# Two outputs by stream at stages' ends, and first outputs one stream after the other, in a two-layer diffusion block

## The chip, the core and the metric

The kernel runs on one core of one Trainium2 chip. The metric is device microseconds for one launch; the median over runs is compared. Engines are named as in the profile: PE is the matrix engine (PEld its weight loads), DVE the vector engine, ACT the scalar engine, POOL the general engine, SP the engine that issues most transfers.

## The reference, cut to what matters

Two layers of a diffusion backbone over 256 context tokens (stream 0) and 256 latent tokens (stream 1), with width 1024. Each layer is a gated feed-forward half step, a mixing step (retention, windowed attention and a recurrent branch, merged and projected) and a second feed-forward half step. Each of the three starts with an RMS norm and a modulation by stream:

```python
def rms_norm(x, w, eps=NORM_EPS):
    xf = x.astype(jnp.float32)
    y = xf * lax.rsqrt(jnp.mean(jnp.square(xf), -1, keepdims=True) + eps)
    return (y * w.astype(jnp.float32)).astype(x.dtype)
def modulate(h, shift, scale):
    return h * (1.0 + scale) + shift
def swiglu(h, w_in, w_out):
    gate, up = jnp.split(h @ w_in, 2, axis=-1)
    return (jax.nn.silu(gate) * up) @ w_out
def ffn_sublayer(x, mod, base, norm_w, w_in, w_out):
    h = modulate(rms_norm(x, norm_w), mod[:, :, base], mod[:, :, base + 1])
    return x + 0.5 * mod[:, :, base + 2] * swiglu(h, w_in, w_out)
```

The output is the latent stream after layer 1.

## The kernel before, in words

Features lie on partitions in 8 tiles of 128 (`KT` = 8); the 512 columns are stream 0 (0 to 255) and stream 1 (256 to 511). A product in float32 is three matmuls on split operands (`mm3`, L185 to L188): high weights by high input, high weights by low input, low weights by high input.

Weights come in tiles of four 128x128 blocks, in the order of a plan (`plan_ffn`, `plan_mix`) that also packs them in memory. `Weights.get` fetches a tile of 256 KB by SP (L113), casts the high part on ACT (L114) and subtracts for the low part on DVE (L115). It keeps the current tile and the one before it; who asks for an older one has it fetched again.

`body` runs three stages for each layer: ffn1 (weights `w0a`, `w1a`), mix (`w0b`, `w1b`) and ffn2 (`w0c`, `w1c`). Both streams go through all of them, but for layer 1's ffn2 and the outputs of its mix, which are latent alone. So four stage ends hand both streams on, and the text calls them E1 (ffn1 to mix in layer 0), E2 (mix to ffn2 in layer 0), E3 (ffn2 of layer 0 to ffn1 of layer 1) and E4 (ffn1 to mix in layer 1).

At a stage's end the last of 8 output tiles goes by stream (`last_out`): 33 matmuls of 256 columns for a stream in a feed-forward stage, 24 in the mix. After each comes the residual on DVE (L373) and the square of that tile (L276). `stats` sums squares by matmuls of one column (L283), takes a root in small DVE steps (L286, L194 to L203) and broadcasts the result over 128 rows by transposes (L290): for stream 0 into `ps_rf`, for stream 1 into `ps_po`. `norm` then makes the inputs of the next stage, for each tile of features and each stream three instructions: u on DVE (L300), the high part of the input on ACT (L302) and the low part on DVE (L303). It takes stream 0's tile kt and then stream 1's tile kt-2.

`first` makes a stage's first outputs (6 tiles in a feed-forward stage, 3 low-rank tiles "lo" in the mix, of which stream 0 of layer 1 has 2) as the inputs come: for each tile of features stream 0's part and, one tile behind, stream 1's with the same weights (L364 with the high input, L369 with the low one).

At the mix's start ACT also casts low-rank weights (`lora`, fetched at L847, cast at L850), whose fetch is held until the last tile of x has been stored (`xd`, L1249).

Each engine's order is not written out: a scheduler with its own timeline model sets it (`TileContext(auto_bufs=True, schedule_with_timeline_sim=True)`).

Of the kernel before, what the change touches and what calls it, by code (L numbers as in the profile page):

```python
# [38 lines left out]
def plan_ffn(wi, wo):  # L39
    out = []  # L40
    for hf in range(2):
        if hf == 0:
            out.append(("first", [(wi, kt, n + p) for kt in range(KT) for p in range(G3) for n in (0, FT)]))
# [3 lines left out]
        for n in range(KT):  # L47
            out.append((f"o{hf}.{n}", fm(wo, n, HF, hf * HF)))
# [9 lines left out]
def plan_mix(l):  # L58
    r0 = RCOL // 128
    out = []  # L60
    for w in ORDER[l].split():
        k, j = w[0], w[1:]
        if w == "lo":
            out.append(("lo", [("mix", kt, r0 + 12 + j) for kt in range(KT) for j in range(3)]))
# [20 lines left out]
    out += [(f"wo{n}", fm("wout", n)) for n in range(KT)]  # L85
    return out
# [36 lines left out]
def body(nc, tc, I, O, es, dbg=None):  # L123
# [684 lines left out]
    def rw_lora(W, H, l, S, st):  # L808
# [4 lines left out]
        first(W, "lo", H, cs, os, 1, 1)  # L813
# [389 lines left out]
    def mix_out(l, W, ms, S, xd):  # L1203
# [21 lines left out]
    for l in range(2):  # L1225
# [15 lines left out]
        W = Weights(nc, mk, I[f"w{l}a"], plan_ffn("f1i", "f1o"))  # L1241
# [17 lines left out]
        W = Weights(nc, mk, I[f"w{l}c"], plan_ffn("f2i", "f2o"))  # L1259
# [49 lines left out]
def arrange(x, c, ctx, c_ctx, ada_w, ada_b, norm_w, ffn1_w_in, ffn1_w_out, ffn2_w_in, ffn2_w_out, mix_w_in,  # L1309
# [55 lines left out]
```

## Time and profile before

| what | value |
|---|---|
| median of 3 runs | 2956.5 us (2952.3 to 2960.07) |
| profiled execution, its own time | 2952.92 us |
| span of its trace | 2951.1 us |
| granted clock of TensorE, mean | 0.963 |
| weight tiles fetched, cast and split | 954 |

The busy shares of the page are averages over the whole span. The change touches four short stretches and the mix behind two of them, so the rows further down are those of the stretches from the end of a stage's last matmul to the last matmul of the next stage's first outputs.

### The profile page before, as it was taken

To read this page: it belongs to the slowest core of one execution; us is meant where nothing else is said; L and a number is where in the kernel's file an instruction comes from. 1 tells how busy PE (TensorE), PEld (TensorE's weight loads), DVE (VectorE), ACT (ScalarE), POOL (GpSimd) and SP (SyncE) were. 2 spreads that over 40 slices of the span, in tenths; PEclk is the share of its full clock that TensorE was granted. 3 is DMA by queue.
4 is the path that set the end of the run, shared out by engine and by line. 5 is a ranking of instruction groups with operands and counts; after the bars stand their busy time and mean duration, and the time that the engine had idled before them with its cause. 6 is when DMAs were issued, how large, how long until landed. Compare 5 with 4: busy or idle time off the path is not lost.

```text
span 2951.1 us, 47422 instructions
## 1 busy us (share of the span) xinstructions
PE 2796.3 (95%) x16761; PEld 2387.8 (81%) x16761; DVE 1999.8 (68%) x4677; ACT 1320.8 (45%) x2968; POOL 375.0 (13%) x1068
## 2 busy tenths in 40 slices
PE   8999999889999999899999999999989898999999
PEld 7888888677877787688888888888878787888999
DVE  7967668666685766467746567455787776577655
ACT  3322245556555654333223332223467665564544
POOL 0000000522032211000000000000033433330000
PEclk9999999889999999999999999999999999799999
DMA  7656444212332146433534435353334233146554
GB/s 268 232 188 192 155 127 132 76 49 82 115 97 78 50 128 216 154 104 126 184 136 162 145 121 173 108 174 120 123 109 112 80 114 113 53 131 202 171 179 154
DMA packets 259727, 400.97 MB, mean 136 GB/s; under 512 B 78752, under 2 KB 96288, under 8 KB 259488
## 3 DMA queue, kind: packets, MB, share of 16 engines
q1 hardware_dynamic: 259488, 397.93, 42.5%
q8 instruction: 132, 2.16, 0.3%
q14 instruction: 107, 0.88, 0.1%
HBM read 368.33 MB, written 25.82 MB: 134 GB/s over the span
## 4 chain that ended last, share of the span: by engine, by line
PE 79%; DVE 6%; POOL 5%; DMA 4%; ACT 2%; issue 2%; SPq 1%; POOLq 0%; DVEq 0%; ACTq 0%
PE ps_mm L186 20%; PE ps_mm L188 20%; PE ps_mm L187 20%; POOL cst L1007 3%; POOL cst L1006 2%; PE ps_mm L364 2%; PE ps_po L774 1%; PE ps_rf L974 1%; DVE wlo L115 1%; PE ps_rx L1084 1%; DMA z<-td 1%; PE ps_po L559 1%; PE ps_rx L1077 1%; PE ps_rx L364 1%; PE ps_rx L1105 1%
## 5 line engine op out<-in xcount | busy, mean ns | idle before, releaser
L114 ACT CAST whi<-raw 128x512 fp32r<-128x512 f32 x954 | 564.6, 617 | 698.9 <-PE ps_mm L187 362.4
L186 PE MATMUL ps_mm<-hall,whi 128*128 128x512 f32 (+1 forms) x2320 | 841.6, 363 | 5.7 <-DVE ft L693 1.5
L188 PE MATMUL ps_mm<-hall,wlo 128*128 128x512 f32 (+1 forms) x2320 | 841.1, 363 | 2.3 <-DVE wlo L115 2.2
L187 PE MATMUL ps_mm<-hall,whi 128*128 128x512 f32 (+1 forms) x2320 | 838.3, 362 | 0.0
L115 DVE TENSOR_TENSOR wlo<-raw,whi 128x512 fp32r<-128x512 f32 x954 | 645.5, 692 | 98.2 <-ACT whi L114 68.4
L186 PEld LDWEIGHTS ps_mm<-hall,whi 128*128 128x128 f32 x2320 | 440.8, 190 | 75.2 <-ACT kv L711 2.0
L188 PEld LDWEIGHTS ps_mm<-hall,wlo 128*128 128x128 f32 x2320 | 439.0, 189 | 75.9 <-DVE wlo L115 4.7
L187 PEld LDWEIGHTS ps_mm<-hall,whi 128*128 128x128 f32 x2320 | 439.7, 190 | 71.3 <-issue 0.3
L186 PE MATMUL ps_mm<-hid,whi 128*128 128x512 f32 (+1 forms) x737 | 260.7, 354 | 0.0
L187 PE MATMUL ps_mm<-hid,whi 128*128 128x512 f32 (+1 forms) x737 | 259.9, 354 | 0.0
L188 PE MATMUL ps_mm<-hid,wlo 128*128 128x512 f32 (+1 forms) x737 | 257.4, 354 | 0.0
L1006 POOL TENSOR_TENSOR cst<-acc,cst 128x60 f32<-128x60 f32 (+24 forms) x496 | 167.9, 339 | 613.7 <-DMA acc<-ad__10934 59.4
L373 DVE SCALAR_TENSOR_TENSOR x<-ps_mm,cst,x 128x256 f32<-128x256 f32 x136 | 61.0, 481 | 193.7 <-PE ps_mm L188 193.6
L401 DVE TENSOR_TENSOR ft<-ft,ps_mm 128x512 f32<-128x512 f32 (+1 forms) x80 | 49.6, 621 | 209.0 <-PE ps_mm L188 199.4
L851 POOL TENSOR_TENSOR ll<-lora,lh 128x512 fp32r<-128x512 f32 x8 | 10.5, 1316 | 1367.9 <-DMA cst<-gup 953.9
L1007 POOL TENSOR_TENSOR cst<-cst 128x60 f32<-128x60 f32 (+24 forms) x496 | 177.2, 357 | 38.0
L236 DVE SCALAR_TENSOR_TENSOR ft<-m,cd 128x1024 bf16<-128x1024 f32 x136 | 163.0, 1221 | 8.7 <-DMA m<-ada 8.7
L237 DVE SCALAR_TENSOR_TENSOR m<-m,cd 128x1024 f32<-128x1024 f32 x136 | 165.6, 1223 | 0.7
L187 PEld LDWEIGHTS ps_mm<-hid,whi 128*128 128x128 f32 x737 | 139.1, 189 | 19.5
L186 PEld LDWEIGHTS ps_mm<-hid,whi 128*128 128x128 f32 x737 | 139.0, 189 | 19.4
L188 PEld LDWEIGHTS ps_mm<-hid,wlo 128*128 128x128 f32 x737 | 138.5, 189 | 19.5
L186 PE MATMUL ps_mm<-whi,hall 128*128 128x256 f32 x416 | 120.7, 291 | 8.2 <-DVE rr_v L799 5.1
(339 smaller groups left out, 4518.7 us busy)
## 6 DMA issues: line engine op xcount, KB each, us to landing
m<-ada SPq DMA_DIRECT2D x136, 512.0 KB, 4.3
raw<-w0b SPq DMA_DIRECT2D x214, 256.0 KB, 2.9
raw<-w1b SPq DMA_DIRECT2D x211, 256.0 KB, 3.1
raw<-w0a SPq DMA_DIRECT2D x132, 256.0 KB, 2.8
raw<-w0c SPq DMA_DIRECT2D x132, 256.0 KB, 4.4
raw<-w1a SPq DMA_DIRECT2D x132, 256.0 KB, 4.3
raw<-w1c SPq DMA_DIRECT2D x132, 256.0 KB, 3.9
gd<-ft SPq DMA_DIRECT2D x24, 256.0 KB, 2.0
```

Source lines behind the costliest of these rows:

```text
L114: nc.scalar.copy(hi, raw)
L115: nc.vector.tensor_sub(lo, raw, hi.bitcast(F32))
L186: PE.matmul(o, w[0], h[0], start=start, stop=False)
L187: PE.matmul(o, w[0], h[1], start=False, stop=False)
L188: PE.matmul(o, w[1], h[0], start=False, stop=stop)
L236: V.scalar_tensor_tensor(junk, raw, 1.0, st["cond"][0], ALU.mult, ALU.mult, accum_out=md[:, kt, 0:1])
L237: V.scalar_tensor_tensor(raw, raw, 1.0, st["cond"][1], ALU.mult, ALU.mult, accum_out=md[:, kt, 1:2])
L364: PE.matmul(o[:, p], w[k, j][q], hl(H[k], p)[0], start=(k == 0 and q == 0 and p.start == c.start), stop=False)
L373: V.scalar_tensor_tensor(xs[n][:, CS[s]], o[:, CS[s]], gate[:, n, s:s + 1], xs[n][:, CS[s]], ALU.mult, ALU.add)
L401: V.tensor_tensor(sg[:, c], sg[:, c], pu[:, c], ALU.mult)
L1006: G.tensor_tensor(w, acc[j // 16][:, j % 16, j + 1:32].unsqueeze(1).to_broadcast([128, m, n]), tt[:, 0:m, j:j + 1].to_broadcast([128, m, n ...
L1007: G.tensor_tensor(tt[:, 0:m, j + 1:32], tt[:, 0:m, j + 1:32], w, ALU.add)
```

## The change

`last_out` becomes `last_outs`: the last two output tiles go by stream, in the order tile 6 stream 0, tile 7 stream 0, tile 7 stream 1, tile 6 stream 1, with stream 0's sums started after the second. `first` for two streams becomes `first2`: all 8 tiles of features of stream 0 for all outputs, then all 8 of stream 1. It is used for ffn2 of layer 0, ffn1 of layer 1 and both "lo"; ffn1 of layer 0 and ffn2 of layer 1 keep `first`. In both, weights are planned and fetched for each pass: tile 6's and the first outputs' twice in the plan, tile 7's again by `Weights.get`. `norm` is unchanged. Line numbers of after are 7 to 27 higher.

```diff
-def plan_ffn(wi, wo):
+def outs(key, tiles, two):
+    if not two:
+        return [(f"{key}{n}", tiles(n)) for n in range(KT)]
+    return [(f"{key}{n}", tiles(n)) for n in list(range(KT)) + [KT - 2]]
...
+    def last_outs(W, key, H, gate):
+
         st["apart"] = True
-        for s in range(2):
+        for n, s in ((KT - 2, 0), (KT - 1, 0), (KT - 1, 1), (KT - 2, 1)):
+            if n < KT - 1 or s == 0:
+                ws = W.take(f"{key}{n}")
             o = ps("mm")
-            for j, w in enumerate(ws):
-                mm3(o[:, CS[s]], w, hl(H[j], CS[s]), j == 0, j == len(ws) - 1)
+            for j, t in enumerate(ws):
+                mm3(o[:, CS[s]], W.get(t), hl(H[j], CS[s]), j == 0, j == len(ws) - 1)
             residual(n, o, gate, (s,))
-            sq_acc(n, (s,))
-            if s == 0:
+            sq_acc(n if s == 0 else 2 * KT - 3 - n, (s,), n)
+            if (n, s) == (KT - 1, 0):
                 stats((0,), "rf")
         st["apart"] = False
+
+    def first2(W, key, H, cs, os):
+
+        bl = W.take(key)
+        for s in range(2):
+            mine = [(o, c) for o, c in zip(os, cs) if c.start <= CS[s].start]
+            n = len(mine)
+            for k in range(KT):
+                for j, (o, c) in enumerate(mine):
+                    mm = W.get(bl[k * n + j])
+                    for q, (w, h) in enumerate(((0, 0), (1, 0), (0, 1))):
+                        PE.matmul(o[:, CS[s]], mm[w], hl(H[k], CS[s])[h], start=(k == 0 and q == 0 and c.start == CS[s].start),
+                                  stop=(k == KT - 1 and q == 2 and s == 1))
+            bl = bl[KT * n:]
...
-        W = Weights(nc, mk, I[f"w{l}a"], plan_ffn("f1i", "f1o"))
+        W = Weights(nc, mk, I[f"w{l}a"], plan_ffn("f1i", "f1o", 1 + l, 2))
...
-        W = Weights(nc, mk, I[f"w{l}c"], plan_ffn("f2i", "f2o"))
+        W = Weights(nc, mk, I[f"w{l}c"], plan_ffn("f2i", "f2o", 2 - l, 2 - l))
```

On PE at E3, the end of ffn2 of layer 0, the sums of squares (`ps_po`, one column each), stream 0's broadcast (`ps_rf`) and the first matmul of the next stage stand so, first before and then after.

```order
L188 MATMUL ps_mm<-hid,wlo 128x256
L283 MATMUL ps_po<-cst,ft 128x1 x4
L290 MATMUL ps_rf<-cst 128x128 x2
L364 MATMUL ps_mm<-hall,whi 128x256
L364 MATMUL ps_mm<-hall,wlo 128x256
```

```order
L195 MATMUL ps_mm<-hid,wlo 128x256
L292 MATMUL ps_po<-cst,ft 128x1 x2
L299 MATMUL ps_rf<-cst 128x128 x2
L292 MATMUL ps_po<-cst,ft 128x1 x2
L369 MATMUL ps_mm<-hall,whi 128x256
L369 MATMUL ps_mm<-hall,wlo 128x256
```

At E3 stream 0's broadcast has moved ahead of the last two of stream 1's sums. At E1, E2 and E4 it has not, as these rows of PE at E1 after the change show:

```order
L194 MATMUL ps_mm<-hid,whi 128x256
L195 MATMUL ps_mm<-hid,wlo 128x256
L292 MATMUL ps_po<-cst,ft 128x1 x4
L299 MATMUL ps_rf<-cst 128x128 x2
L369 MATMUL ps_mm<-hall,whi 128x256
```

On DVE at E1, behind stream 1's broadcast, the u instructions of both streams (`ft<-x,cst,ps_po` is stream 1's, `ft<-x,cst,ps_rf` stream 0's) and the low parts of the inputs (`hall`) stand so before, from the eighth u on:

```order
L300 SCALAR_TENSOR_TENSOR ft<-x,cst,ps_rf 128x256
L303 SCALAR_TENSOR_TENSOR hall<-ft,cst,hall 128x256 x6
L115 TENSOR_TENSOR wlo<-raw,whi 128x512
L303 SCALAR_TENSOR_TENSOR hall<-ft,cst,hall 128x256
L300 SCALAR_TENSOR_TENSOR ft<-x,cst,ps_po 128x256
L303 SCALAR_TENSOR_TENSOR hall<-ft,cst,hall 128x256
L300 SCALAR_TENSOR_TENSOR ft<-x,cst,ps_rf 128x256
L300 SCALAR_TENSOR_TENSOR ft<-x,cst,ps_po 128x256 x3
```

And after, from the same place:

```order
L309 SCALAR_TENSOR_TENSOR ft<-x,cst,ps_rf 128x256
L312 SCALAR_TENSOR_TENSOR hall<-ft,cst,hall 128x256 x4
L122 TENSOR_TENSOR wlo<-raw,whi 128x512
L312 SCALAR_TENSOR_TENSOR hall<-ft,cst,hall 128x256 x3
L309 SCALAR_TENSOR_TENSOR ft<-x,cst,ps_po 128x256
L312 SCALAR_TENSOR_TENSOR hall<-ft,cst,hall 128x256
L309 SCALAR_TENSOR_TENSOR ft<-x,cst,ps_rf 128x256
L309 SCALAR_TENSOR_TENSOR ft<-x,cst,ps_po 128x256 x3
L122 TENSOR_TENSOR wlo<-raw,whi 128x512
L312 SCALAR_TENSOR_TENSOR hall<-ft,cst,hall 128x256
L122 TENSOR_TENSOR wlo<-raw,whi 128x512
L312 SCALAR_TENSOR_TENSOR hall<-ft,cst,hall 128x256 x4
```

DVE's list has hardly moved: stream 1's inputs are still made between those of stream 0, while PE now wants stream 1's only after all of stream 0's.

On ACT at E1, around the first high part of an input (`hall`), the casts of low-rank weights (`lh`) stand so, before and after:

```order
L850 CAST lh<-lora 128x512
L302 ACTIVATE hall<-ft,cst 128x256 x3
L850 CAST lh<-lora 128x512
L302 ACTIVATE hall<-ft,cst 128x256 x8
L114 CAST whi<-raw 128x512
```

```order
L877 CAST lh<-lora 128x512
L121 CAST whi<-raw 128x512
L877 CAST lh<-lora 128x512
L311 ACTIVATE hall<-ft,cst 128x256 x3
L121 CAST whi<-raw 128x512 x2
```

The second cast of `lora`, which stood behind three high parts, now stands ahead of the first.

## Rows read from the trace of the kernel before

**Rows 1.** The page's head and its busy times by engine.
```profile
span 2951.1 us, 47422 instructions
...
PE 2796.3 (95%) x16761; PEld 2387.8 (81%) x16761; DVE 1999.8 (68%) x4677; ACT 1320.8 (45%) x2968; POOL 375.0 (13%) x1068
```
**Rows 2.** Busy by stretch, E1 to E4: length, PE, PEld, DVE, ACT, POOL, clock, DMA, GB/s.
```profile
405.42:431.42 26.00, 21.57 (x159) 20.47 (x158) 20.34 (x58) 10.70 (x24) 2.54 (x2) 0.87 0.39 117
1318.08:1361.00 42.92, 39.12 (x306) 38.12 (x305) 26.26 (x72) 15.12 (x31) 0.00 (x0) 0.96 0.15 47
1694.87:1738.13 43.26, 38.72 (x302) 37.52 (x301) 25.72 (x68) 14.38 (x30) 0.00 (x0) 0.96 0.23 74
2072.01:2097.92 25.91, 20.75 (x135) 19.59 (x133) 20.14 (x58) 11.50 (x25) 2.54 (x2) 0.74 0.49 158
```
**Rows 3.** Timeline of PE at E1: start, length, instruction, wait before it and its releaser.
```profile
407.17 0.61 PE L283 MATMUL ps_po<-cst,ft 128*128 128x1 f32 x4 [1.24 <-DVE ft L276]
...
410.47 0.58 PE L364 MATMUL ps_mm<-hall,whi 128*128 128x256 f32 x1 [1.67 <-ACT hall L302]
410.85 0.41 PE L364 MATMUL ps_mm<-hall,wlo 128*128 128x256 f32 x1
...
412.98 0.41 PE L364 MATMUL ps_ap<-hall,wlo 128*128 128x256 f32 x1
...
413.83 0.63 PE L290 MATMUL ps_po<-cst 128*128 128x128 f32 x2
415.58 0.39 PE L364 MATMUL ps_mm<-hall,whi 128*128 128x256 f32 x1 [1.12 <-ACT hall L302]
```
**Rows 4.** Timeline of PE ahead of E1, where the form of the matmuls changes.
```profile
395.95 0.39 PE L186 MATMUL ps_mm<-hid,whi 128*128 128x512 f32 x1
396.18 0.39 PE L187 MATMUL ps_mm<-hid,whi 128*128 128x512 f32 x1
...
396.74 0.28 PE L187 MATMUL ps_mm<-hid,whi 128*128 128x256 f32 x1
396.86 0.28 PE L188 MATMUL ps_mm<-hid,wlo 128*128 128x256 f32 x1
```
**Rows 5.** Timeline of DVE at E1, behind stream 1's broadcast.
```profile
414.50 0.48 DVE L300 SCALAR_TENSOR_TENSOR ft<-x,cst,ps_po 128x256 f32<-128x256 f32 x1 [1.66 <-PE ps_po L290]
414.90 0.47 DVE L300 SCALAR_TENSOR_TENSOR ft<-x,cst,ps_rf 128x256 f32<-128x256 f32 x1
...
417.64 2.46 DVE L303 SCALAR_TENSOR_TENSOR hall<-ft,cst,hall 128x256 fp32r<-128x256 f32 x6
420.01 0.69 DVE L115 TENSOR_TENSOR wlo<-raw,whi 128x512 fp32r<-128x512 f32 x1
420.62 0.48 DVE L303 SCALAR_TENSOR_TENSOR hall<-ft,cst,hall 128x256 fp32r<-128x256 f32 x1
```
**Rows 6.** The page's groups by line: a weight tile's cast and its subtraction.
```profile
L114 ACT CAST whi<-raw 128x512 fp32r<-128x512 f32 x954 | 564.6, 617 | 698.9 <-PE ps_mm L187 362.4
...
L115 DVE TENSOR_TENSOR wlo<-raw,whi 128x512 fp32r<-128x512 f32 x954 | 645.5, 692 | 98.2 <-ACT whi L114 68.4
```
**Rows 7.** Timeline of SP and ACT at E1: the low-rank weights, issued and cast.
```profile
406.52 0.42 SPq L847 DMA_DIRECT2D lora<-lora  x1
...
409.39 0.62 ACT L850 CAST lh<-lora 128x512 fp32r<-128x512 f32 x1 [5.94 <-DMA lora<-lora]
...
412.49 0.62 ACT L850 CAST lh<-lora 128x512 fp32r<-128x512 f32 x1 [1.28 <-DMA lora<-lora]
```
**Rows 8.** Timeline of PE: the first matmul behind E2, E3 and E4.
```profile
1323.02 0.58 PE L364 MATMUL ps_mm<-hall,whi 128*128 128x256 f32 x1 [1.11 <-ACT hall L302]
...
1698.89 0.58 PE L364 MATMUL ps_mm<-hall,whi 128*128 128x256 f32 x1 [1.12 <-ACT hall L302]
...
2078.09 0.58 PE L364 MATMUL ps_mm<-hall,whi 128*128 128x256 f32 x1 [2.39 <-ACT hall L302]
```
**Rows 9.** Waits of PE by releaser: total us, times, longest; the recurrent branch's chain.
```profile
PE ps_rx L1033 <- DVE rb L1021: 11.3, 2, 7.5
```
**Rows 10.** Busy by stretch inside E4, columns as in rows 2.
```profile
2084.00:2086.00 2.00, 2.00 (x11) 2.00 (x11) 2.00 (x7) 1.05 (x3) 0.00 (x0) 0.50 0.08 30
2086.00:2088.00 2.00, 2.00 (x13) 2.00 (x13) 2.00 (x7) 0.34 (x1) 0.00 (x0) 0.60 0.75 221
```

More of the change, by code (lines that the diff above doesn't have):

```diff
@@ L42, in plan_ffn @@
         if hf == 0:
-            out.append(("first", [(wi, kt, n + p) for kt in range(KT) for p in range(G3) for n in (0, FT)]))
+            out.append(("first", [(wi, kt, n + p) for kt in range(KT) for p in range(G3) for n in (0, FT)] * rounds))
         for p in range(hf * HF + (0 if hf else G3), hf * HF + HF):
@@ L46, in plan_ffn @@
             out.append((f"u{p}", fm(wi, FT + p)))
-        for n in range(KT):
-            out.append((f"o{hf}.{n}", fm(wo, n, HF, hf * HF)))
+        out += outs(f"o{hf}.", lambda n: fm(wo, n, HF, hf * HF), hf == 1 and parts == 2)
     return out
@@ L63, in plan_mix @@
         if w == "lo":
-            out.append(("lo", [("mix", kt, r0 + 12 + j) for kt in range(KT) for j in range(3)]))
+            lo = [("mix", kt, r0 + 12 + j) for kt in range(KT) for j in range(3)]
+            out.append(("lo", (lo if l == 0 else [b for b in lo if b[2] < r0 + 14]) + lo))
             if l > 0:
@@ L84, in plan_mix @@
     out += [(f"bw{n}", fm("wrw", n, 4)) for n in range(KT)]
-    out += [(f"wo{n}", fm("wout", n)) for n in range(KT)]
-    return out
+    return out + outs("wo", lambda n: fm("wout", n), l == 0)
 class Weights:
@@ L389, in ffn @@
                 os = [ps(t) for t in ("mm", "mm", "rx", "rx", "ap", "sc")[:2 * G3]]
-                first(W, "first", H, [c] * len(os), os, 1 if lead and len(S) == 2 else 0)
+                if lead and len(S) == 2:
+                    first2(W, "first", H, [c] * len(os), os)
+                else:
+                    first(W, "first", H, [c] * len(os), os)
             for j in range(HF):
@@ L408, in ffn @@
             for n in range(KT):
-                if hf == 1 and n == KT - 1 and len(S) == 2:
-                    last_out(W, f"o{hf}.{n}", hid, gate)
+                if hf == 1 and n >= KT - 2 and len(S) == 2:
+                    if n == KT - 2:
+                        last_outs(W, f"o{hf}.", hid, gate)
                     run(1)
@@ L812, in rw_lora @@
         cs, os = (full, full, span(S)), [ps(t) for t in ("mm", "mm", "ap")]
-        first(W, "lo", H, cs, os, 1, 1)
+        first2(W, "lo", H, cs, os)
         for j, (c, o) in enumerate(zip(cs, os)):
@@ L1210, in mix_out @@
         for n in range(KT):
-            if n == KT - 1 and len(S) == 2:
-                last_out(W, f"wo{n}", ms, gate)
-                continue
+            if n == KT - 2 and len(S) == 2:
+                last_outs(W, "wo", ms, gate)
+                break
             o = ps("mm")
```

17 lines of the change are left out of this document (8 added, 9 removed).

## The prediction

> **What bounds the kernel now.** I read the page's busy times first: PE is busy for 95% of the span and DVE for 68% [rows 1]. An average like that says only that PE is what most stretches wait for; what a change of order can win has to be looked for where PE has nothing to do. So I cut out the four stage ends that the change touches, each from the end of a stage's last matmul, called T0 here, to the end of the last matmul of the next stage's first outputs [rows 2]. They last 26.0, 42.9, 43.3 and 25.9 us, 138.1 together. What PE has to do in them is known: 6 outputs of 8 tiles in 3 products for 2 streams are 288 matmuls of 256 columns in E2 and E3; 3 outputs are 144 in E1, and 120 in E4, where stream 0 has 2 outputs. At full clock such a matmul starts 0.119 us after the one before (the two starts at 396.74 and 396.86, [rows 4]), so the work is 34.3, 34.3, 17.1 and 14.3 us. The rest, 8.6, 9.0, 8.9 and 11.6 us or 38 in all, is the most that any order of these stretches can give back: 1.3% of the time.
>
> Then the timelines, to see where that loss lies. It has two parts. The first is the restart, from T0 to the first matmul: 5.05 us in E1 (410.47 less 405.42, [rows 2, 3]), 4.94, 4.02 and 6.08 in the others [rows 8]. In it stand the last residual, the last square, a wait of PE for that square (1.24 us in E1, [rows 3]), the sums, the root, the broadcast, u, and the high part on ACT. In E1 the last thing to come is on ACT: the first high part stands behind a cast of low-rank weights, which ended an idle time of 5.94 us for a transfer issued at 406.52 [rows 7]. The second part is slow work behind the restart. PE runs at half clock there, a matmul each 0.213 us (ten steps from 410.85 to 412.98), and it waits once more for inputs behind stream 1's broadcast (1.12 us at 415.58, [rows 3]). DVE is what feeds it: each tile and stream costs DVE a u of 0.40 us and a low part of 0.395 (six in 417.64 to 420.01), and a weight tile 0.61 (420.01 to 420.62, [rows 5]). DVE is busy for 20.3 of E1's 26.0 us, but only 26 of some 43 in E2 and E3, where PE's own work is longer [rows 2].
>
> **The change part by part.** *The last two outputs by stream.* Splitting a matmul of 512 columns in two costs 2 x 0.119 - 0.227 = 0.011 us [rows 4]. The order of the changed kernel has 123 fewer of 512 and 246 more of 256, so this costs 1.35 us. The Trainium skill, "TensorE: Matmul & The Clock Gate", section "Back-to-back issue gap", gives the isolated gap at full clock as N/2.4 + 2.5 ns, 216 and 109 ns here; by it the splits would cost some 0.3 us, an estimate from that page. The trace's 0.227 and 0.119 us are a little longer, and the sum keeps its own 1.35.
>
> What the split could win is an earlier broadcast of stream 0: its sums are ready one output before T0. But PE works in its order, and in E1, E2 and E4 that broadcast still stands behind all four of stream 1's sums, which wait for the last residual and square. So nothing of that wait goes there. What does come earlier in E2 is stream 0's root, whose small steps no longer mix with stream 1's; I take E2's restart as E3's today, 4.1 us instead of 4.94. In E3 the broadcast has moved ahead of the last two sums; it loses the wait for the square and what is mixed in with it, and I take 2.65 instead of 4.02. In E1 and E4 the second cast of low-rank weights now stands ahead of the first high part. Its transfer is issued behind the store of the last tile of x, at about T0 + 1.1 as the first one's is today (406.52), and lands 2.9 (409.39) to 4.0 us (412.49) later [rows 7], so at T0 + 4.0 to 5.1. With 0.5 for the cast and 0.6 from a high part to PE's start the restart would be 5.1 to 6.2; I take 5.2, and 6.1 in E4, which are the early bounds, since fewer transfers are issued beside it.
>
> *First outputs one stream after the other.* PE would now need stream 0's inputs at one tile for each 9 matmuls (1.07 us) in E1, 6 in E4 and 18 (2.14 us) in E2 and E3. But DVE's list is nearly what it was: behind stream 1's broadcast it does 8 alternating u, then low parts and u of both streams, with the subtractions of weight tiles between. PE can't pass from stream 0 to stream 1 before DVE has come to stream 0's last low part, and by then DVE has also made nearly all of stream 1's inputs. So stream 1's pass, half of the work, starts after what was before nearly all of DVE's list, and then runs with nothing to wait for. Before, both streams' matmuls filled DVE's pace.
>
> E1, from its order: restart 5.2; the 27 matmuls up to stream 1's broadcast, 15 at half clock and 12 at full, 4.6; broadcast and start of DVE 0.6; DVE to stream 0's last low part, 13 u (13 x 0.39 = 5.1), 10 low parts (4.0) and 3 weight tiles (1.8), 10.9; the 3 matmuls that this frees 0.4; stream 1's pass 72 x 0.119 = 8.6. Sum 30.3, against 26.0: +4.2. E4 in the same way: 6.1 + 18 matmuls 3.6 + 0.6 + 10.3 (13 u, 10 low parts, 2 weight tiles) + 0.2 + 65 matmuls 7.7 = 28.5, against 25.9: +2.6. E2: 4.1 + 32 matmuls 5.2 + 0.6 + 15.8 (13 u, 12 low parts, 7 weight tiles, then 14 matmuls) + 144 x 0.119 = 17.1 make 42.8, against 42.9: -0.1. E3: 2.65 + 33 matmuls 4.6 (between 5.3 and 3.9, as half the clock lasts) + 0.6 + 15.9 + 17.1 = 40.9, against 43.3: -2.4. The four together: +4.3.
>
> *Weights fetched twice.* 54 tiles more (954 to 1008), each a transfer of 256 KB, a cast of 0.62 us and a subtraction of 0.69 [rows 6]. What lies in DVE's lists is in the sums above. The rest lies beside PE's work: in stream 1's pass PE takes 12 matmuls, 1.43 us, for each tile, and DVE, with its inputs done, needs 0.61. That is 183 GB/s of fetching, where the stretch of E4 already moves 158 on average [rows 2]. Taken as 0.
>
> *The mix behind E1 and E4.* PE waits there twice, 11.3 us together, for a chain of the recurrent branch that runs on POOL [rows 9]; fourteen more such chains are covered by PE's work. The scheduler moved some of that cover. I take 0; the bounds are losing or gaining as much as those two waits, 11 us either way.
>
> Sum: 4.3 + 1.35 = +5.7 us on the profiled execution's 2952.9 (span 2951.1 and 1.8 around it), so 2958.6. That execution lies 3.6 under the median of 2956.5, so I forecast 2962.
>
> **The rivals.** *Cover lost in the mix* (slower). One more chain of the recurrent branch shows, or the two show for longer, by as much as they do now: 2962 + 11 = 2973. It decides when a stretch of PE's work in front of such a chain's first consumer shrinks by more than its slack. For it: in about 10 of 16 chains the work there is less, by 1 to 9 us; against it: most are covered by more.
>
> *Stream 0's pass at PE's pace* (faster). If DVE, with both broadcasts early, keeps ahead, a stretch is its restart, PE's own work and some 2 us of half clock and broadcast: 5.2 + 17.1 + 2.1 = 24.4 in E1, and by the same 40.3, 38.2 and 22.4 in the others, together 125.3 against 138.1, so -12.8 + 1.4 = -11.4: 2945. Against it stands DVE's fixed list; for it, that u and low parts could be shorter when less runs beside them.
>
> *Half clock for longer* (slower). PE's granted clock is half behind each restart, and in E4, where a second wait follows, it stays at half until about 2087 (0.50 and 0.60, [rows 10]), 13 us behind T0. If short bursts between waits keep it there through stream 0's pass, its 111 matmuls behind the broadcast take 111 x 0.213 = 23.6 us instead of 15.8 in E2 and E3: +15.6, 2978. The Trainium skill's same page, section "HAM oscillation — how this bites in real kernels", tells that bursts between waits let the clock drop again; E4's rows agree. Against it: E2 and E3, the long ones, had 0.96 on average [rows 2].
>
> *Weights late* (slower). If the doubled fetches come too late in two of four passes by some 5 us each, which is seven subtractions of 0.69 us [rows 6] that PE would stand and wait for: 2972. The transfers speak against it: they ran at up to 158 GB/s on average in E4 without PE waiting for one [rows 2].
>
> *Nothing happens*: losses and gains of the four ends cancel and the time is within 0.3% (8.9 us) of 2956.5, which is about what a measurement tells from no change. My forecast lies inside this too.
>
> **How the numbers follow.** Forecast case 0.5 (2955 to 2969, as E1's and E4's restarts and E3's gain vary), cover lost 0.15, PE's pace 0.18, half clock 0.08, weights late 0.05, cover gained in the mix 0.04 (2951). Within 0.3% means 2947.6 to 2965.4. Faster: most of PE's pace, 0.15, and most of cover gained, 0.03: 0.18. Slower: the three slower rivals, 0.28, and the upper end of the forecast case, 0.09: 0.37. Same: 0.45. The range runs from 2947 to 2975, which leaves half of PE's pace (0.09) below and half clock (0.08) above.
>
> **What would show it.** In the changed trace: E1 and E4 longer by 2 to 5 us, with PE in stream 0's pass waiting for `hall` again and again and stream 1's pass at 0.12 us a matmul without a wait; E3 shorter with a restart under 3 us; E2 about the same; 0.01 us for each split. Wrong would be: stream 0's pass without waits; weight tiles (`whi`, `wlo`) as releasers of PE in the second pass; a granted clock of half through a pass; another total of the waits for the recurrent branch's chains.

## The result, and the profile after

The changed kernel takes 2979.2 us (median of 4 runs, 2970.8 to 2980.7) against 2954.4: a ratio of 1.0086, with an interval of 1.0066 to 1.0107. It is slower by 25 us, where the prediction had 2962 and a range that ended at 2975. The page's head and busy times, which answer to [rows 1]:

```profile
span 2976.6 us, 47879 instructions
...
PE 2807.5 (94%) x16884; PEld 2401.1 (81%) x16884; DVE 2025.8 (68%) x4735; ACT 1335.5 (45%) x3026; POOL 376.4 (13%) x1068
```

PE is busy for 11 us more, but the span has grown by 25.5: 14 us of what was lost is waiting. To see where, I cut both traces at the same places: the four stage ends, as in [rows 2], and the two mixes between them, from the last of E1's (E4's) first outputs to the mix's last matmul. First the changed kernel, in the order E1, mix of layer 0, E2, E3, E4, mix of layer 1, columns as in [rows 2]:

```profile
406.24:438.70 32.46, 24.63 (x158) 23.64 (x157) 25.65 (x71) 15.01 (x31) 2.54 (x2) 0.79 0.49 158
438.70:1332.72 894.02, 827.25 (x5039) 682.48 (x5038) 594.52 (x1567) 453.63 (x1111) 180.88 (x530) 0.94 0.35 106
1332.72:1374.62 41.90, 38.38 (x303) 37.44 (x302) 31.73 (x75) 20.26 (x42) 0.00 (x0) 0.96 0.37 114
1708.95:1749.98 41.03, 38.53 (x303) 37.58 (x301) 31.41 (x72) 20.55 (x42) 0.00 (x0) 0.96 0.55 179
2086.53:2116.62 30.09, 21.40 (x134) 19.82 (x133) 24.22 (x69) 13.87 (x29) 2.67 (x2) 0.77 0.56 184
2116.62:2775.59 658.97, 601.44 (x4535) 532.15 (x4532) 480.91 (x1294) 396.05 (x1010) 190.11 (x530) 0.92 0.39 116
```

and the two mixes of the kernel before:

```profile
431.41:1318.08 886.67, 824.55 (x5010) 680.88 (x5009) 595.18 (x1557) 454.53 (x1107) 180.56 (x530) 0.95 0.36 106
2097.92:2749.58 651.66, 598.10 (x4534) 528.81 (x4532) 480.62 (x1295) 398.75 (x1010) 189.18 (x530) 0.93 0.40 117
```

The lines show three shares. The ends: 32.5, 41.9, 41.0 and 30.1 us, 145.5 against 138.1, so +7.4; E1 and E4 lost 6.5 and 4.2, E2 and E3 won 1.0 and 2.2. The mixes, which the change hardly touches (29 matmuls more in the first, from its last outputs by stream): +7.4 and +7.3. And the feed-forward stretches between, which the same cut gives:

```profile
70.53:406.24 335.71, 335.05 (x1517) 274.85 (x1516) 252.39 (x479) 100.94 (x182) 0.00 (x0) 1.00 0.58 189
1374.62:1708.95 334.33, 334.33 (x1517) 274.64 (x1516) 216.21 (x384) 99.94 (x180) 0.00 (x0) 1.00 0.49 168
1749.98:2086.53 336.55, 334.95 (x1516) 274.81 (x1515) 201.03 (x381) 99.54 (x181) 0.00 (x0) 1.00 0.44 146
```

Before they were 334.0, 333.9 and 333.9 us with PE busy throughout; the first and the third of them:

```profile
71.42:405.42 334.00, 334.00 (x1483) 272.95 (x1482) 250.49 (x477) 98.29 (x176) 0.00 (x0) 1.00 0.58 187
...
1738.13:2072.01 333.88, 333.88 (x1484) 272.88 (x1482) 199.18 (x377) 98.05 (x173) 0.00 (x0) 1.00 0.44 147
```

So they took +1.7, +0.5 and +2.7, and in the first and third PE is no longer busy throughout. (The first outputs of the program end 0.9 us earlier.)

E1 can be read against the prediction's sum. PE's timeline shows its first matmul, stream 1's broadcast and the waits behind it, and the windows show E1 from the first matmul to the end of stream 0's pass, and stream 1's pass:

```profile
412.45 0.58 PE L369 MATMUL ps_mm<-hall,whi 128*128 128x256 f32 x1 [1.99 <-ACT hall L311]
...
418.18 0.38 PE L299 MATMUL ps_po<-cst 128*128 128x128 f32 x2
420.08 0.39 PE L369 MATMUL ps_mm<-hall,whi 128*128 128x256 f32 x1 [1.51 <-ACT hall L311]
...
420.77 0.28 PE L369 MATMUL ps_ap<-hall,wlo 128*128 128x256 f32 x1
422.67 0.80 PE L369 MATMUL ps_mm<-hall,whi 128*128 128x256 f32 x2 [1.62 <-DVE hall L312]
...
424.12 0.41 PE L369 MATMUL ps_mm<-hall,wlo 128*128 128x256 f32 x1
```

```profile
412.45:430.00 17.55, 14.42 (x74) 13.81 (x75) 15.10 (x38) 9.77 (x22) 0.89 (x1) 0.65 0.21 54
430.00:438.70 8.70, 8.70 (x74) 8.70 (x74) 5.13 (x9) 3.01 (x5) 0.00 (x0) 1.00 0.77 247
```

The restart is 6.21 us (412.45 less 406.24), the matmuls up to the broadcast take 5.73, DVE's list 11.8 (418.18 to 430.00) and stream 1's pass 8.7 at full clock. The prediction had 5.2, 4.6, 11.9 and 8.6. Behind the wait at 422.67 PE ran on at half clock (0.41 us a matmul at 424.12, 0.28 at 420.77) until about 428; it came to stream 0's last tile at 429.60, just behind DVE's last low part for it (429.5), so DVE's list set that end.

### The profile page after: what moved, and what is told of

Same layout as the page of the kernel before. It is cut to its first block, busy times and chain, and to the rows that moved or that the text cites. A ratio compares the mean times of both kernels' runs of the same rounds, so it can differ in the third digit from the quotient of the medians.

```text
span 2976.6 us, 47879 instructions
## 1 busy us (share of the span) xinstructions
PE 2807.5 (94%) x16884; PEld 2401.1 (81%) x16884; DVE 2025.8 (68%) x4735; ACT 1335.5 (45%) x3026; POOL 376.4 (13%) x1068
## 3 DMA queue, kind: packets, MB, share of 16 engines
q1 hardware_dynamic: 267264, 411.90, 43.3%
## 4 chain that ended last, share of the span: by engine, by line
PE 76%; DVE 8%; POOL 6%; DMA 4%; ACT 3%; issue 2%; SPq 1%; DVEq 0%; POOLq 0%; ACTq 0%
PE ps_mm L195 19%; PE ps_mm L193 19%; PE ps_mm L194 19%; POOL cst L1034 3%; POOL cst L1033 3%; PE ps_mm L369 1%; DVE wlo L122 1%; PE ps_rf L1001 1%; PE ps_rx L1111 1%; DMA z<-td 1%; PE ps_rx L1104 1%; PE ps_po L586 1%; PE ps_po L801 1%; PE ps_rx L1060 1%; PE ps_rx L1115 1%
## 5 line engine op out<-in xcount | busy, mean ns | idle before, releaser
L121 ACT CAST whi<-raw 128x512 fp32r<-128x512 f32 x1008 | 587.5, 617 | 439.4 <-PE ps_mm L194 235.5
L122 DVE TENSOR_TENSOR wlo<-raw,whi 128x512 fp32r<-128x512 f32 x1008 | 676.2, 690 | 48.6 <-ACT whi L121 31.8
L193 PE MATMUL ps_mm<-hid,whi 128*128 128x512 f32 (+1 forms) x770 | 266.0, 346 | 0.0
L194 PE MATMUL ps_mm<-hid,whi 128*128 128x512 f32 (+1 forms) x770 | 265.7, 347 | 0.0
L195 PEld LDWEIGHTS ps_mm<-hid,wlo 128*128 128x128 f32 x770 | 144.5, 189 | 20.4 <-DVE wlo L122 2.5
L193 PEld LDWEIGHTS ps_mm<-hid,whi 128*128 128x128 f32 x770 | 145.5, 189 | 18.4
L194 PEld LDWEIGHTS ps_mm<-hid,whi 128*128 128x128 f32 x770 | 145.5, 189 | 18.2
L217 ACT CAST hid<-ft 128x512 fp32r<-128x512 f32 (+1 forms) x88 | 50.1, 571 | 225.4 <-DVE ft L427 225.4
```

Source lines behind the costliest of these rows:

```text
L121: nc.scalar.copy(hi, raw)
L122: nc.vector.tensor_sub(lo, raw, hi.bitcast(F32))
L193: PE.matmul(o, w[0], h[0], start=start, stop=False)
L194: PE.matmul(o, w[0], h[1], start=False, stop=False)
L195: PE.matmul(o, w[1], h[0], start=False, stop=stop)
L217: A.copy(dst[0], src)
```

## The experiments

Theory A is the prediction's account of the ends (DVE's order decides). For the mix there were first M1 (the scheduler's order, which any change may turn, sets its length) and M2 (the low-rank outputs by stream do), later theory B. The table has for each kernel the median, the median of the kernel before in the same comparison, the ratio with its interval, and from one profile the lengths of the six stretches, cut as above; e10 to e12 are one run each.

| kernel | us | before | ratio | E1 | mix 0 | E2 | E3 | E4 | mix 1 |
|---|---|---|---|---|---|---|---|---|---|
| before | | | | 26.0 | 886.7 | 42.9 | 43.3 | 25.9 | 651.7 |
| before, again (e12) | 2955.1 | 2954.8 | one run | 26.6 | 889.0 | 42.9 | 43.2 | 24.7 | 652.9 |
| changed | 2979.2 | 2954.4 | 1.0086 (1.0066 to 1.0107) | 32.5 | 894.0 | 41.9 | 41.0 | 30.1 | 659.0 |
| changed, again (e11) | 2976.5 | 2954.8 | one run | 32.7 | 898.0 | 43.2 | 39.5 | 29.8 | 653.7 |
| e1 | 2945.9 | 2950.3 | 0.9985 (0.9971 to 0.9998) | 28.0 | 880.1 | 43.7 | 41.6 | 26.9 | 644.6 |
| e2 | 2955.4 | 2950.3 | 1.0015 (0.9999 to 1.0031) | 31.8 | 887.3 | 43.1 | 42.7 | 27.9 | 644.8 |
| e3 | 2954.8 | 2950.3 | 1.0009 (0.9993 to 1.0025) | 29.1 | 880.2 | 42.1 | 41.1 | 26.1 | 657.1 |
| e4 | 2948.7 | 2950.3 | 1.0003 (0.9989 to 1.0016) | 27.6 | 886.9 | 41.0 | 39.2 | 29.7 | 649.8 |
| e5 | 2949.4 | 2951.8 | 0.9986 (0.9964 to 1.0009) | 27.4 | 883.6 | 44.6 | 43.6 | 25.1 | 648.6 |
| e6 | 2972.0 | 2951.8 | 1.0066 (1.0040 to 1.0092) | 34.3 | 891.0 | 42.0 | 41.0 | 30.9 | 648.8 |
| e7 | 2947.4 | 2951.8 | 0.9986 (0.9966 to 1.0005) | 26.3 | 890.0 | 40.9 | 39.2 | 24.6 | 643.1 |
| e8 | 2958.8 | 2951.8 | 1.0024 (1.0005 to 1.0042) | 30.1 | 883.6 | 42.2 | 41.0 | 27.0 | 657.6 |
| e9 | 2963.8 | 2954.8 | 1.0033 (1.0015 to 1.0050) | 25.5 | 894.0 | 40.7 | 39.2 | 23.7 | 663.9 |
| e10 | 2973.9 | 2954.8 | one run | 35.6 | 884.7 | 43.0 | 41.0 | 33.7 | 653.7 |
| e13 | 2957.4 | 2949.0 | 1.0028 (1.0011 to 1.0045) | 31.6 | 883.5 | 42.9 | 39.5 | 28.9 | 649.8 |
| e14 | 2927.0 | 2949.0 | 0.9934 (0.9912 to 0.9956) | 25.5 | 878.0 | 41.8 | 39.1 | 24.2 | 635.4 |
| e15 | 2924.1 | 2949.0 | 0.9918 (0.9903 to 0.9933) | 25.6 | 879.6 | 41.0 | 39.2 | 24.5 | 633.9 |
| e16 | 2933.1 | 2948.8 | 0.9947 (0.9930 to 0.9963) | 26.8 | 879.9 | 44.8 | 43.6 | 24.7 | 635.2 |

### The change in parts: e1 to e4

e1 keeps the last outputs by stream and takes all first outputs as before; e2 is the reverse; e3 leaves the change out of the low-rank outputs alone. Their diffs against the changed kernel take back these lines (cut; the marks behind # are added here):

```diff
-        first2(W, "lo", H, cs, os)                               # e1, e3
+        first(W, "lo", H, cs, os, 1, 1)
...
-                    first2(W, "first", H, [c] * len(os), os)     # e1
...
+                first(W, "first", H, [c] * len(os), os, 1 if lead and len(S) == 2 else 0)
...
-                        last_outs(W, f"o{hf}.", hid, gate)       # e2, also in mix_out
+                    last_out(W, f"o{hf}.{n}", hid, gate)
```

> Only the last two outputs go by stream; all first outputs are those of before. Theory A (the ends: DVE makes both streams' inputs in turn, so taking stream 0's first outputs alone lengthens E1 and E4): E1 and E4 fall back from 32.5 and 30.1 us to 26 to 27 each, E2 and E3 stay at 42 to 43, so the four ends are within 1 us of before's 138. Of the mix, where the change lost 7.4 us behind E1 and 7.3 behind E4, two theories: M1, that any change of the program makes the scheduler shuffle the mix, expects each of the two stretches to differ from before's 886.7 and 651.7 by several us, of either sign; M2, that the loss comes from the low-rank outputs by stream, expects both within 1 us of before. Total: M1 between -10 and +15, M2 within 3 us of before.

> Only the first outputs go one stream after the other; the last outputs are those of before. Theory A: E1 and E4 stay long (32 and 30 us), E2 41 to 43, and E3 loses its earlier broadcast, so 42 to 43 against 41.0. M2 expects the mix to lose 7 us twice as in the changed kernel (894 and 659); M1 expects other numbers than in the changed kernel, of any sign. Total: M2 +22 against before, M1 between 0 and +25.

> The change without its low-rank part: the mix's low-rank outputs are taken as before, with both streams interleaved and each weight fetched once. Theory A: E1 26 to 27 and E4 26 to 27 us, E2 41.9 and E3 41.0 as in the changed kernel, so the ends are 2 to 3 us under before. M2: the mix is back at 886.7 and 651.7, and the kernel is at before's time or up to 3 us under it. M1: the mix differs from both kernels, and the total lies anywhere from -8 to +15.

e4 is the changed kernel with the norm written out in another order:

```diff
-            for kt in range(KT + 2):
-                if kt < KT:
-                    modulate(kt, 0, ft())
-                if kt == 1:
-                    stats((1,), "po")
-                if kt >= 2:
-                    modulate(kt - 2, 1, ft())
+            for kt in range(KT):
+                modulate(kt, 0, ft())
+            stats((1,), "po")
+            for kt in range(KT):
+                modulate(kt, 1, ft())
```

> The change, with the norm written out so that all 8 tiles of stream 0 are modulated ahead of stream 1's. DVE's order then has the 8 u and 8 low parts of stream 0 first. Theory A: PE no longer waits for stream 1's u in stream 0's pass. E1 28 us against 32.5, E4 27 against 30.1, E2 41, E3 39 to 40: the ends 7 to 9 us under the changed kernel. The rival, that PE's half clock or late weights hold the passes up, expects E1 and E4 to stay over 30. The mix: M2 expects 894 and 659 as in the changed kernel, M1 anything from -8 to +8 around that.

Of the ends theory A holds in the main. With first outputs by stream (e2) E1 is 31.8 us and E4 27.9 (30 expected); without them (e1, e3) E1 is 28.0 and 29.1, a little over what was expected, since the restart stayed long there; e8 tells why. With DVE's order turned, E1 falls from 32.5 to 27.6 and E3 from 41.0 to 39.2, as forecast; E4 (29.7 instead of 27) is a miss, and e4's trace names most of it: behind a wait of 1.62 us at 2091.11 PE ran some 27 matmuls of stream 1's pass at half clock (0.50 granted from 2091.10 to 2095.00), an estimated 27 x (0.213 - 0.119) = 2.5 us, while in its E1 the clock was full from 420 on. Of the mix M2 falls: e2, which has the low-rank outputs by stream, has mixes of 887.3 and 644.8, not 894 and 659, and e3, which doesn't, has 657.1 in layer 1. e1 and e3 have the same order of PE's rows in the mix of layer 0, row for row, and the same length within 0.1 us (880.1 and 880.2).

### Does the mix move by itself? e5, e6, e10 to e12

e5 (of before) and e6 (of the changed kernel) add one instruction whose result nobody reads behind each mix's norm, e10 adds eight to the changed kernel (the mark behind # is added here); e11 and e12 are the two kernels unaltered, profiled again.

```diff
         H = norm(l, 1, 3, both)
+        for nul in range(1):     # 8 in e10
+            V.tensor_tensor(ft(), xs[nul], xs[nul], ALU.mult)
```

> The kernel before, with one spare DVE instruction of 128 by 512 elements (some 0.7 us) behind the norm of each mix, whose result nobody reads. By itself it is worth at most 0.7 us twice. M1 (the mix's length follows from how the scheduler happens to interleave it) expects the two mix stretches to move by 2 to 8 us each from before's 886.7 and 651.7, of either sign, with the four ends within 2 us of 138.1. M2 (the loss in the mix belongs to the low-rank outputs by stream) expects both within 1 us of before.

> The changed kernel with the same spare DVE instruction. M1 expects the mix stretches to move by several us from 894.0 and 659.0, and more likely down, since both were the longest seen; the ends within 2 us of 145.5. M2 expects 894 and 659 within 1 us, so no change in the total beyond 1.5 us.

> The changed kernel with eight spare DVE instructions behind the norm of each mix instead of one. It has nearly the changed kernel's order in the mix (in PE's rows of the second mix 62 of 3678 differ, in the first 364 of 4046; with one spare instruction it was 1485 and 2269). M1, that the order sets the mix's length, expects the second mix at 659.0 within 1.5 us and the first at 894.0 within 4, though more spare work is in it; the rival, that spare work or chance of the run moves the mix, expects 5 us or more of difference in either. The ends grow by up to 5 us twice (8 x 0.7 on DVE).

> The changed kernel, unaltered, profiled once more: how far one execution's stretches differ from another's. M1 needs the two mix stretches within 2 us of 894.0 and 659.0; if they lie 5 us away, differences of that size between kernels mean nothing.

> The kernel before, unaltered, profiled once more, for the same purpose: 886.7 and 651.7 within 2 us, and the ends at 138.1 within 1, if the order sets them; otherwise the spread of one execution.

With a useless instruction of 0.7 us the mixes were 3.1 and 3.1 us shorter in e5 and 3.0 and 10.2 in e6; the ends grew by 2.6 and 2.7 us. But two profiles of one kernel differ by up to 4.0 and 5.3 us in a mix as well (894.0 and 898.0, 659.0 and 653.7), more than I had asked for, so single differences of that size say little. The traces tell what the 5.3 us are: with PE's rows in the same order, one stretch of the second mix took 16.6 us in the changed kernel and 11.1 in e11 (from 2224.06 to 2240.66, and from 2227.84 to 2238.95), at a granted clock of 0.51 in the one and 1.00 in the other:

```profile
2224.00:2241.00 17.00, 16.94 (x115) 13.97 (x115) 13.13 (x51) 9.61 (x33) 0.57 (x2) 0.51 0.34 96
2227.80:2239.00 11.20, 9.72 (x113) 8.07 (x114) 9.62 (x35) 9.48 (x33) 0.00 (x0) 1.00 0.34 95
```

Over both profiles the change costs 8.2 us in the first mix (896.0 against 887.9) and 4.0 in the second (656.3 against 652.3); in the second pair alone it is 9.0 and 0.8. So a loss in the first mix repeats, and one in the second is not shown.

e10 was a clear miss in the first mix: 884.7 with nearly the changed kernel's order. But its rows on PE differ from the changed kernel's at one place near 560 us and then only between 1046 and 1227 us. From the same row of PE to the same row these are, in the changed kernel, in e11 and in e10:

```profile
1046.06:1227.23 181.17, 171.62 (x977) 138.15 (x976) 105.10 (x240) 76.02 (x185) 19.91 (x62) 0.97 0.51 165
1052.57:1232.28 179.71, 170.91 (x977) 137.81 (x975) 105.30 (x240) 76.02 (x185) 19.91 (x62) 0.97 0.51 165
1052.47:1223.90 171.43, 168.65 (x977) 137.17 (x975) 104.30 (x240) 75.92 (x185) 19.75 (x62) 0.98 0.54 175
```

The same 977 matmuls take 8 to 10 us less in e10's order. That is as much as the first mix lost, and it is what M1 says, for this stretch.

What repeats is single waits. The waits of PE over 2.2 us, listed by place, hold one of 6.4 us at 1137, in that stretch, in the changed kernel that neither e10 nor before has; e11 has it at the same place (6.3), e9 too (6.1), and e6 one of 4.3. These four have the longest first mixes of the table, 891.0 to 898.0. Here it is in the changed kernel, first on PE, then what DVE did meanwhile:

```profile
1137.24 0.77 PE L1104 MATMUL ps_rx<-cst,gk 128*128 128x128 f32 x2 [6.44 <-DVE rb L1138]
```

```profile
1130.07 0.29 DVE L1137 COPY rb<-ps_rx 64x128 f32<-64x128 f32 x1
1135.55 0.43 DVE L1052 STREAM_TRANSPOSE tg<-z 32x256 f32<-32x256 f32 x1 [5.18 <-DMA z<-td]
1136.01 0.29 DVE L1137 COPY rb<-ps_rx 64x128 f32<-64x128 f32 x1
1136.34 0.43 DVE L1052 STREAM_TRANSPOSE tg<-z 32x256 f32<-32x256 f32 x1
1136.80 0.50 DVE L1138 TENSOR_TENSOR rb<-rb,ps_rx 64x128 f32<-64x128 f32 x2
```

PE waits for L1138, the last step of one recurrent chain. In front of it in DVE's order stands L1052, which reads the next chain's result z, and that is still on its way through memory from POOL: DVE stands 5.2 us for a transfer, and everything behind it with it. The second mix has the same on ACT, where an attention step (`ae`) stands behind a copy of z (L1051) that waited 5.5 us, and PE waits 6.6 us for it:

```profile
2542.57 0.40 ACT L1051 COPY tg<-z 32x256 f32<-32x256 f32 x1 [5.46 <-DMA z<-td]
...
2544.55 0.67 ACT L792 ACTIVATE ae<-ps_sc,cst 128x512 f32<-128x512 f32 x1
```

```profile
2545.36 1.11 PE L798 MATMUL ps_ap<-cst,ae 128*128 128x128 f32 x4 [6.55 <-ACT ae L792]
```

The kernel before has a wait of that size in its second mix too (6.8 us at 2508), and e10 has this one (6.1) with a second mix of 653.7, so it is not what separates the kernels there.

That gave theory B: readers of z that stand ahead of their transfer block the queue behind them.

### Tile 7's weights: e8

```diff
-                ws = W.take(f"{key}{n}")
+                ws = [W.get(t) for t in W.take(f"{key}{n}")]
             o = ps("mm")
-            for j, t in enumerate(ws):
-                mm3(o[:, CS[s]], W.get(t), hl(H[j], CS[s]), j == 0, j == len(ws) - 1)
+            for j, w in enumerate(ws):
+                mm3(o[:, CS[s]], w, hl(H[j], CS[s]), j == 0, j == len(ws) - 1)
```

> The changed kernel, with tile 7's weights taken once for both streams, as the kernel before does, in place of fetched again for stream 1. In the changed kernel the stretches ahead of E1 and E4 are 1.7 and 2.7 us longer, with waits of PE for a weight tile's low part (0.5 and 1.4 us). If the fetch again is the cause, these shrink to 0.5 to 1 us over before and the waits are gone; if the order by stream itself is, they stay. The mix: M1 lets it move, M2 holds it at 894 and 659.

The stretches ahead of E1 and E4 are 334.6 and 334.3 us instead of 335.7 and 336.6, with PE busy throughout, so the fetch again cost 1.1 and 2.2 us there. What I had not expected is that E1 and E4 shrank by 2.4 and 3.1 us as well: their restarts are 3.67 us instead of 6.21 and 7.05. In PE's rows of e8 stream 0's broadcast stands ahead of stream 1's last sums there, and the first matmul follows at 409.46, with T0 at 405.79:

```profile
406.16 0.41 PE L299 MATMUL ps_rf<-cst 128*128 128x128 f32 x2
408.53 0.89 PE L292 MATMUL ps_po<-cst,ft 128*128 128x1 f32 x4 [1.96 <-DVE ft L285]
409.46 0.58 PE L369 MATMUL ps_mm<-hall,whi 128*128 128x256 f32 x1
```

In the changed kernel the same broadcast came at 410.05, since DVE finished the root late: constants of the mix, which are held until the stage's last weight fetch has been issued, and that fetch had become a late one (issued at 375.9 in the kernel before, 383.1 in e8 and 389.9 in the changed kernel), stood in its order between the steps (here L514 and L433), and the second cast of low-rank weights stood ahead of the first high part:

```profile
407.64 0.42 DVE L514 TENSOR_SCALAR dt<-ph,cst 128x384 f32<-128x384 f32 x1
...
408.38 1.27 DVE L433 TENSOR_SCALAR cst<-cst 128x16 f32<-128x16 f32 x1
409.56 0.15 DVE L209 SCALAR_TENSOR_TENSOR cst<-cst 128x2 f32<-128x2 f32 x1
```

```profile
411.37 0.62 ACT L877 CAST lh<-lora 128x512 fp32r<-128x512 f32 x1 [2.58 <-DMA lora<-lora]
```

### Keeping what pays: e7 and e9

e7 uses the change only ahead of feed-forward stages (E2, E3), with e4's norm there and e1's `first` for "lo". e9 has the last outputs by stream at all four ends with e8's weights, and the rest as e7. Of e7's diff, the norm (the mark behind # is added here):

```diff
-            for kt in range(KT + 2):
+            lag = 2 if j == 1 else KT        # j == 1: the mix's norm
+            for kt in range(KT + lag):
```

> The parts of the change where they paid: stream 0's first outputs alone and its inputs first on DVE only ahead of a feed-forward stage (E2, E3), the last two outputs by stream only there too; E1, E4 and the low-rank outputs as before. Theory A: E1 26.0 and E4 25.9 as before, E2 41 and E3 39 to 40, the ends 132 to 133 against 138.1; the feed-forward stretches ahead of E1 and E4 back at 334.0 and 333.9. So 5 us under before, apart from the mix, which M1 lets move by up to 7 us twice and M2 holds at before's.

> Everything that paid at an end: last two outputs by stream at all four ends with tile 7's weights kept, first outputs by stream and inputs of stream 0 first on DVE only ahead of feed-forward stages, low-rank outputs as before. Theory A: restarts of 3.7 us at E1 and E4 and the rest of these stretches as before (21 and 20 us), so E1 24.6, E4 23.5, E2 41, E3 39.2: 128 against 138.1; the feed-forward stretches 0.5 us longer each. The mix: M1 gives it yet another order, so anything from -8 to +8 in each stretch; M2 before's 886.7 and 651.7. Total -8 by M2.

The ends came out as forecast: 131.0 us in e7 (132 to 133 expected) and 129.0 in e9 (128 expected), 7 and 9 us under before. e7 is level with before, e9 is 9 us slower than before, though its ends are the best of all: its mixes are 7.4 and 12.3 us longer. This is the plainest sight of the case. The ends do what theory A says, and the mixes take it back, of which up to some 5 us each lies within what two profiles of one kernel differ by.

### Readers behind their chain: e13 to e16

These put the readers of z, on DVE and ACT, behind the steps of the chain ahead of them: e13 in the changed kernel, e14 in e9, e15 in e7, e16 in the kernel before. The diff, cut:

```diff
-        V.transpose(fl(tn), fl(z[0:32, 0]))
+        with tc.issue_after(st["lv"]) if "lv" in st else nullcontext():
+            V.transpose(fl(tn), fl(z[0:32, 0]))
...
-            A.copy(tu[0][bs, :, bs], z[bs, 0])
-            V.transpose(tu[1][bs, :, bs], z[bs, 1])
+            with tc.issue_after(st["la"]) if "la" in st else nullcontext():
+                A.copy(tu[0][bs, :, bs], z[bs, 0])
+            with tc.issue_after(st["lv"]) if "lv" in st else nullcontext():
+                V.transpose(tu[1][bs, :, bs], z[bs, 1])
...
-                A.copy(ve[d][64:128, q], x[64:128, 128:256])
+                st["la"] = A.copy(ve[d][64:128, q], x[64:128, 128:256]).ins
...
-                        V.tensor_tensor(ya[64:128, q], ya[64:128, q], x[64:128, 384:512], ALU.add)
+                        st["lv"] = V.tensor_tensor(ya[64:128, q], ya[64:128, q], x[64:128, 384:512], ALU.add).ins
```

> The changed kernel, where the instructions that read the recurrent chain's result z from memory (two DVE transposes and the ACT copies of each merge) must stand, in DVE's and ACT's order, behind the steps of the chain ahead of them. In the changed kernel a transpose of the next chain stands in front of a DVE step of the present one and waits 5.2 us for the transfer of z, and PE waits 6.4 us for that step. Theory B (a reader ahead of its transfer blocks the queue behind it): that wait of PE at the last part of the first mix is gone and the first mix is 5 to 7 us shorter than 894.0 (897 in its other profile), if the new order brings no other wait of that size; the wait of 6.6 us for an attention step behind an ACT copy in the second mix may stay, since that step is not part of a chain. The rival, that the length is set by the amount of work on PE, DVE or POOL: 894 and 659 within the 5 us by which two profiles of one kernel differ.

> The kernel with everything that paid at an end (ends 129.0), with the same rule for the readers of z. It had the same wait of 6.1 us late in the first mix (894.0) and one of 7.0 us in the second (663.9). Theory B: the first is gone, the first mix is 5 to 7 us shorter, the ends stay at 129 within 1.5. Rival as in the run before.

> The kernel with the change only ahead of feed-forward stages, with the same rule for the readers of z. It has no such wait late in the first mix (890.0 and 643.1, ends 131.0). Theory B expects no gain of that kind here: the mix within 5 us of that, of either sign, and the total near 2947. The rival that the rule itself speeds the mix expects both mixes shorter by 3 us or more.

> The kernel before, with only the rule for the readers of z. The ends stay at 138 within 1.5 us and the feed-forward stretches as before. Theory B with what e14 and e15 showed: the waits of PE of over 5 us late in the mix (6.8 at an L1077 of the second mix) go, DVE and ACT wait some 40% less for z, and the mix is 8 us or more shorter in the first and 10 or more in the second, total 15 to 25 under before. Rival, that the mix of before was not held up by this: within 5 us of 886.7 and 651.7.

In e13 the 6.4 us wait is gone, the first mix is 10.5 us shorter (883.5), and the kernel is at 1.0028 of before where it was at 1.0086. DVE's rows at that place show the chain's last steps done one after the other, with no transpose between:

```profile
1133.03 0.29 DVE L1140 COPY rb<-ps_rx 64x128 f32<-64x128 f32 x1
1133.35 0.29 DVE L1141 TENSOR_TENSOR rb<-rb,ps_rx 64x128 f32<-64x128 f32 x1
1133.81 0.29 DVE L1140 COPY rb<-ps_rx 64x128 f32<-64x128 f32 x1 [0.16 <-PE ps_rx L1135]
1134.13 0.29 DVE L1141 TENSOR_TENSOR rb<-rb,ps_rx 64x128 f32<-64x128 f32 x1
```

e14 and e15 gained more than theory B had asked for: in e15, where no such wait stood late in the first mix, I had expected none, and the rival (the rule itself speeds the mix) was right: 10.4 and 9.2 us. That fits blocked queues costing time in many small places, not only in the one that I had found; the rule also reorders other rows, and no run parts the two. e16 shows the same in the kernel before: its mixes fall by 6.8 us (8 expected) and 16.5, and the kernel to 2933.1, a ratio of 0.9947. In the second of them PE is busy for 8.8 us less with as many matmuls (589.3 against 598.1), at a granted clock of 0.95 instead of 0.93, so about half of that gain is the clock. The waits of ACT and DVE for z, by line, in the kernel before and in e16:

```profile
ACT tg L1024 <- DMA z<-td: 58.6, 20, 10.1
DVE tg L1025 <- DMA z<-td: 41.9, 12, 7.1
DVE rb L1021 <- DMA z<-td: 6.6, 1, 6.6
```

```profile
ACT tg L1026 <- DMA z<-td: 39.9, 12, 11.7
DVE tg L1028 <- DMA z<-td: 10.3, 2, 7.5
DVE rb L1022 <- DMA z<-td: 7.4, 3, 3.8
```

From 107.1 to 57.6 us. In the changed kernel, without the rule, they are:

```profile
ACT tg L1051 <- DMA z<-td: 61.8, 18, 9.8
DVE tg L1052 <- DMA z<-td: 27.3, 8, 5.5
DVE rb L1048 <- DMA z<-td: 21.4, 6, 5.6
```

Together 110.5 us (99.6 in e11), no more than in the kernel before (107.1, and 108.5 in e12). So these waits are a cost of both kernels and their total does not separate them: with the rule in both, e13 is still 24 us above e16.

e15 is the best version: 2924.1 us, 0.9918 (0.9903 to 0.9933) of before; of its 25 us the rule gives about 16 (e16) and the change where it pays the other 9, though alone, in e7, that gave 4.4 us, not clear of none.

## Why the prediction was wrong

**The step that failed** is the one on the mix: "I take 0; the bounds are losing or gaining as much as those two waits, 11 us either way". The two mixes took +7.4 and +7.3 in the profile that the result is read from (+8.2 and +4.0 over two profiles of each), the largest part of the 25 us. The bound was made from one kind of wait, the chain on POOL that PE's work must cover. That was the rival "cover lost", priced at 2973; the waits of that kind grew from 11.3 [rows 9] to 14.8 us in this pair of profiles and from 12.1 to 12.5 in the other, so they are not it. In the first mix the runs show in its place the order of the rows between 1046 and 1227 us: the changed kernel takes 8 to 10 us more there than e10, and 6.4 of it is PE's wait for a DVE step that stands behind a reader of z. No row of PE's waits names that, since it shows the step that came last, not what it stood behind. In the second mix 5.5 of the 7.3 us are the granted clock of one execution. What the change costs there stays open: 0.8 us in the other pair of profiles, but 14.6 between e16 and e13, which both have the rule.

**The second failure** is "Taken as 0" for weights fetched twice. In stream 1's passes PE's work does cover the transfers; but tile 7's fetch again cost 3.3 us ahead of E1 and E4 (e8) and moved the release of the mix's constants and the order of the sums, another 5.5 in E1 and E4 together. That is 8.8 us, near the 10 of the rival "weights late", with another mechanism.

**Mis-sized terms.** For the restarts of E1 and E4 I took the early bounds, 5.2 and 6.1; they were 6.21 and 7.05, at the late bound of 6.2 in E1, since the second low-rank weights landed at T0 + 5.1 (411.37). Of the 27 matmuls ahead of the broadcast 24 ran at half clock, where I had taken 15: 5.73 us instead of 4.6. The clock then rose, and in the wait of 1.62 us before 422.67 it fell to half, 1.2 GHz, once more; from 412.45 to 430.00 the grant is 0.65 on average. The Trainium skill, "TensorE: Matmul & The Clock Gate", section "HAM oscillation — how this bites in real kernels", has it that bursts with waits between them let the clock drop again; E1 agrees. (The rows of E4 [rows 10], which the prediction put beside that section, show the clock staying at half, not falling anew.) In E2 and E3 it did not bite: 0.96 in both, as before.

**What held.** That stream 1's broadcast and DVE's list decide E1: 11.8 us against 11.9 worked out, and 8.7 against 8.6 for the pass behind it; e4 showed it by turning DVE's order, and e7 and e9 did so in E2 and E3. E2 (41.9 against 42.8) and E3 (41.0 against 40.9, restart 2.61 against 2.65) came close; that E3 agrees to 0.1 us is luck, since e11 has 43.2 and 39.5, with granted clocks of 0.92 and 1.00. The split's cost: 0.45 us in the stretch ahead of E3, against 33 x 0.011 = 0.4. Two slips in the prediction hardly move it: 2087 is 15 us behind E4's T0, not 13, and with 2.1 us in each end "PE's pace" adds up to 126.4 us, not 125.3.

What stays open: why the scheduler placed the readers of z so in one kernel and otherwise in another (its timeline is not in a trace), and the second mix.

## What to carry to other kernels

Where a scheduler orders the engines, the price of a change also lies in stretches that it does not touch; cut both traces at the same places before a total is explained, and profile one kernel twice to know which differences count, with the granted clock beside each. A reader of a slow transfer that stands in an engine's order ahead of ready work blocks that work; look for waits of DVE and ACT for a DMA, not only for those of PE, and tie such a reader behind the work that must not wait. Taking one stream's outputs first wants the engine that makes the inputs to take that stream first too: with both, E2 and E3 fell to 41.0 and 39.2 us (e4), while E1, at 27.6, was still above before's 26.0.

## What the runs showed that I had not expected

One spare instruction of 0.7 us changed thousands of rows of PE's order (e6). Two profiles of one program differ by 4 to 5 us in a mix, and where I could place it that was the granted clock: 16.6 us at 0.51 and 11.1 at 1.00 for the same rows. And a rule of a few lines, which keeps two engines from standing at a transfer, was worth 16 us by itself in a kernel that was thought tuned (e16).
